# Numbering the rows of a batch by 16 x partition + column, with fewer one-tile loads, in an argmax, gather and scatter kernel

## The chip, the cores and the metric

The kernel runs on one core of one Trainium2 chip. Times are device microseconds of that core, and all runs told here are in the fast state or, where one is a single look, of unknown state. Ratios are the mean time of one kernel's fast runs over the mean of the other's in the same rounds, with a 95% interval, so they are not quite the ratios of the medians quoted beside them. The reported time is about 1.8 us longer than the span of the profile of the same run.

## The reference

```python
B, S, H = 8, 2048, 2560            # scores (B, S, S), values (B, S, H), float32, fixed seed
best_j = np.argmax(scores, axis=2)
gathered = values[b_idx, best_j, :]
out = np.zeros_like(values)
np.add.at(out, (b_idx, best_j), gathered)
```

(The lines are shortened.) Row j of a batch of the output is therefore values[j] times the number of score rows that have their largest element in column j. Rows with a count of 1 are copied, rows with 0 are zeroed, rows with 2 or more are multiplied. In the fixed draw there are 5,875, 6,131 and 4,378 of them over the eight batches.

## The kernel before

VectorE finds the argmax of each row of scores, TensorE counts the columns by one-hot products, and the output is written by indirect DMAs that GpSimd issues, 128 rows each. The count of row j stands in `cnt[p, t]`, at j = 128 t + p.

```python
row_i = consts.tile([P, NT], INT32)                       # row of cnt[p, t]
nc.gpsimd.iota(row_i[:], pattern=[[P, NT]], base=0, channel_multiplier=1)
# ... how many tiles of scores one load takes
most_n = 1 if x < 2 or turn <= x < 3 * NT else 2 if x < 4 or turn <= x < 5 * NT else R
# ... count_steps
lo = am & (P - 1)      # partition p of the count
hi = am >> 7           # column t
# ... rows with count 1: one DMA per column t straight from values to out;
# partitions whose count is not 1 get an index out of bounds and are skipped
def copy_once(t):
    free_running(scatter_rows_in_dram(
        nc, out_flat[:, :], values[b, t * P:(t + 1) * P, :], one_i[:, t:t + 1], last_row))
first = (NT, 6, 4)[min(b, 2)]      # copies issued in a row at the head of a batch
for t in range(first):
    copy_once(t)
# ... rows with 0 and with 2 or more get a rank (running number by partition, then
# column), are put into lists of 128, and list place v goes to the engine v mod 16
def gathers():                      # 5 lists; then scaled by ScalarE and scattered
    for k in range(MCAP):
        gather(v, mi[:, k:k + 1]); scale(v)
        if rest: copy_once(rest.pop(0))
def zeros(columns):                 # 7 lists (12 in the last batch) from a row of zeros
    for k in columns:
        scatter(zrow[:], zi[:, k:k + 1], free_running)
        if rest: copy_once(rest.pop(0))
```

The cuts are marked by dots, and two calls are abbreviated. In the last batch `level_engines` deals the zero rows out so that all sixteen DMA engines get about the same number of row packets in all.

## Time and profile before

| what | before |
|---|---|
| time, median of 4 runs | 827.3 us (826.99 to 827.59) |
| span of the profiled run, whose own time was 829.2 us | 827.4 us |
| moved by DMA | 347.04 MB |
| VectorE busy | 679 us, finished at 697 us |
| row packets (10,240 B) in the trace | 20,762, mean 387.4 ns, median 385 ns |

The lines of the profile stand in the prediction. In the lines with windows the columns are: the window and its length in us, busy us with the number of instructions for each engine, the granted clock, the DMA share of sixteen engines, and GB/s. The trace also records single DMA packets; I call "excess" what packets took beyond the median of their size, summed and divided by 16, which is the time it costs if it falls on all engines alike.

### The profile page before, as it was taken

What the parts mean: (1) busy time and instruction counts of PE and PEld (TensorE: products, weight loads), DVE (VectorE), ACT (ScalarE), POOL (GpSimd) and SP (SyncE); (2) the same over time, 40 slices, a digit from 0 to 9 for tenths busy, and PEclk for the clock granted to TensorE, in tenths of its full rate; (3) what the DMA queues carried; (4) which work ended last, traced back from release to release, by engine and by line L of the source; (5) the groups of instructions that cost most, each with busy time, mean ns of one, the idle gap of its engine ahead of it and who ended that gap; (6) DMA issues with size and microseconds to landing.
All of it is one profiled execution on the core that took longest, in us unless ns stands there. A gap on an engine that the chain in (4) does not pass through costs nothing.

```text
span 827.4 us, 2091 instructions
## 1 busy us (share of the span) xinstructions
PE 14.7 (2%) x273; PEld 14.2 (2%) x273; DVE 679.0 (82%) x794; ACT 100.7 (12%) x43; POOL 273.0 (33%) x277
## 2 busy tenths in 40 slices
PE   0000000000000000000000000000000000000000
PEld 0000000000000000000000000000000000000000
DVE  7999999999999999999999999999999995000000
ACT  1000000320230000230002300002300320230230
POOL 0000641257004141042250140530416365455451
DMA  9999999999999999999999999999999999999996
GB/s 380 437 423 421 404 404 430 424 424 403 425 428 427 428 424 427 427 427 438 418 429 430 425 428 434 417 429 429 435 422 422 423 427 418 425 424 415 423 426 277
DMA packets 48112, 347.04 MB, mean 419 GB/s; under 512 B 19014, under 2 KB 19014, under 8 KB 19014
## 3 DMA queue, kind: packets, MB, share of 16 engines
q0 software_dynamic: 38736, 212.67, 62.0%
q1 hardware_dynamic: 9360, 134.22, 38.1%
q14 instruction: 14, 0.11, 0.0%
q8 instruction: 2, 0.03, 0.0%
HBM read 354.42 MB, written 300.15 MB: 791 GB/s over the span
## 4 chain that ended last, share of the span: by engine, by line
DVE 81%; DMA 12%; issue 3%; POOL 2%; PE 0%; POOLq 0%; DVEq 0%
DVE am L198 37%; DVE mx L197 34%; DMA room<-in_values_dram,many_i 7%; DMA out_dram<-room,many_i 4%; DVE oh_lo L205 3%; DVE oh L332 2%; POOL out_dram L171 1%; POOL out_dram L33 1%; DVE lo L201 1%; DMA room<-in_scores_dram 1%; DVE oh_hi L209 1%; POOL room L166 0%; DVE hi L203 0%; DVE rank L322 0%; DVE put L347 0%
## 5 line engine op out<-in xcount | busy, mean ns | idle before, releaser
L197 DVE MAX8 mx<-room 128x8 f32<-128x2048 f32 x128 | 291.7, 2279 | 4.5 <-DMA room<-in_scores_dram 4.5
L198 DVE FIND_INDEX8 am<-mx,room 128x8 uint32<-128x2048 f32 x128 | 292.5, 2285 | 0.0
L371 ACT ACTIVATE room<-room,many_c 128x2560 f32<-128x2560 f32 x40 | 96.6, 2426 | 694.3 <-DMA room<-in_values_dram,many_i 694.3
L33 POOL DMA_INDIRECT out_dram<-in_values_dram,ones_i x128 | 130.5, 1020 | 130.0 <-DVE m L303 91.6
L171 POOL DMA_INDIRECT out_dram<-room,many_i x40 | 38.9, 974 | 235.9 <-ACT room L371 233.3
L166 POOL DMA_INDIRECT room<-in_values_dram,many_i x40 | 42.7, 1067 | 152.9 <-DMA out_dram<-room,many_i 79.0
L171 POOL DMA_INDIRECT out_dram<-zrow,zero_i x61 | 59.8, 980 | 18.6 <-issue 18.6
L205 DVE TENSOR_TENSOR oh_lo<-lo,lane_f 128x512 bf16<-128x512 uint32 x32 | 22.2, 694 | 0.3
L332 DVE TENSOR_TENSOR oh<-lo,fill_f 128x2048 f16<-128x2048 uint32 x8 | 18.3, 2292 | 0.3
L213 PE MATMUL cnt_ps<-oh_hi,oh_lo 128*128 128x16 bf16 x128 | 8.2, 174 | 572.9 <-DVE oh_hi L209 558.2
L213 PEld LDWEIGHTS <-oh_lo 128*128 128x128 bf16 x128 | 8.4, 105 | 572.7 <-DVE oh_lo L205 571.6
L198 DVE MATCH_VALUE_LOAD am<-mx,room 128x8 f32 x128 | 11.8, 92 | 4.3
L209 DVE TENSOR_TENSOR oh_hi<-hi,lane_f 128x64 bf16<-128x64 uint32 x32 | 7.0, 218 | 0.0
L201 DVE TENSOR_SCALAR lo<-am 128x4 uint32<-128x4 uint32 x32 | 5.7, 177 | 1.1
L350 PE MATMUL l_ps<-put,oh 128*128 128x32 f16 x128 | 4.7, 188 | 73.1 <-DVE put L347 73.1
L350 PEld LDWEIGHTS <-oh 128*128 128x128 f16 x128 | 4.7, 104 | 74.2 <-DVE oh L332 63.8
L203 DVE TENSOR_SCALAR hi<-am 128x4 uint32<-128x4 uint32 x32 | 5.6, 174 | 0.0
L337 DVE TENSOR_TENSOR ez<-hi,lane_f 128x256 f16<-128x256 uint32 x8 | 3.3, 418 | 0.0
L347 DVE TENSOR_TENSOR put<-ez,row_f 128x256 f16<-128x256 f16 x8 | 3.3, 418 | 0.0
L359 DVE TENSOR_SCALAR e<-l_ps 128x32 f32<-128x32 f32 x8 | 1.5, 185 | 2.0 <-PE l_ps L350 2.0
L322 DVE TENSOR_SCALAR rank<-base,off_ps 128x16 f32<-128x16 f32 x16 | 3.0, 232 | 0.0
L345 DVE TENSOR_TENSOR put<-em,row_f 128x128 f16<-128x128 f16 x8 | 2.3, 292 | 0.3
(88 smaller groups left out, 52.5 us busy)
## 6 DMA issues: line engine op xcount, KB each, us to landing
room<-in_scores_dram SPq DMA_DIRECT2D x13, 4096.0 KB, 48.8
room<-in_scores_dram SPq DMA_DIRECT2D x24, 2048.0 KB, 12.3
room<-in_scores_dram SPq DMA_DIRECT2D x28, 1024.0 KB, 10.6
out_dram<-in_values_dram,ones_i POOLq DMA_INDIRECT x128
out_dram<-zrow,zero_i POOLq DMA_INDIRECT x61
room<-in_values_dram,many_i POOLq DMA_INDIRECT x40
out_dram<-room,many_i POOLq DMA_INDIRECT x40
```

The lines of the kernel that those rows point to most:

```text
L33: return eng.add_instruction(ins)
L166: note(nc.gpsimd.indirect_dma_start(out=v, out_offset=None, in_=values_flat[:, :], in_offset=bass.IndirectOffsetOnAxis(ap=idx, axis=0), bo ...
L171: note(nc.gpsimd.indirect_dma_start(out=out_flat[:, :], out_offset=bass.IndirectOffsetOnAxis(ap=idx, axis=0), in_=v, in_offset=None, bound ...
L197: nc.vector.max(out=mx[:], in_=rows)
L198: nc.vector.max_index(out=am[:, g, :], in_max=mx[:], in_values=rows)
L201: nc.vector.tensor_single_scalar(out=lo[:], in_=am[:, :, 0], scalar=P - 1, op=ALU.bitwise_and)
L205: nc.vector.tensor_tensor(out=oh_lo[:], in0=lo[:].unsqueeze(2).to_broadcast([P, G, P]), in1=lane_f[:].unsqueeze(1).to_broadcast([P, G, P]) ...
L209: nc.vector.tensor_tensor(out=oh_hi[:], in0=hi[:].unsqueeze(2).to_broadcast([P, G, NT]), in1=lane_f[:, 0:NT].unsqueeze(1).to_broadcast([P, ...
L213: nc.tensor.matmul(out=cnt_ps[:], lhsT=oh_lo[:, k, :], rhs=oh_hi[:, k, :], start=(t == G - 1 and k == 0), stop=(t == NT - 1 and k == G - 1))
L332: nc.vector.tensor_tensor(out=oh[:], in0=lo[:].unsqueeze(2).to_broadcast([P, NT, P]), in1=fill_f[:].unsqueeze(1).to_broadcast([P, NT, P]), ...
L350: nc.tensor.matmul(out=l_ps[:], lhsT=oh[:, t, :], rhs=put[:, t, :], start=(t == 0), stop=(t == NT - 1))
L371: nc.scalar.activation(out=v, in_=v, func=mybir.ActivationFunctionType.Copy, bias=0.0, scale=mc[:, k:k + 1])
```

## The change

The intent: rows that follow each other in a list should also lie next to each other in memory, the copies should spread over memory, and fewer loads should be of one tile only.

```diff
-    nc.gpsimd.iota(row_i[:], pattern=[[P, NT]], base=0, channel_multiplier=1)
+    nc.gpsimd.iota(row_i[:], pattern=[[1, NT]], base=0, channel_multiplier=NT)
...
-        most_n = 1 if x < 2 or turn <= x < 3 * NT else 2 if x < 4 or turn <= x < 5 * NT else R
+        most_n = 1 if x < 2 or 2 * NT - 2 <= x < 3 * NT - 4 else 2 if x < 4 or turn <= x < 5 * NT else R
...
-  lo: in_=am[:, :, 0], scalar=P - 1, op=ALU.bitwise_and
+  lo: in_=am[:, :, 0], scalar=4, op=ALU.logical_shift_right
-  hi: in_=am[:, :, 0], scalar=7, op=ALU.logical_shift_right
+  hi: in_=am[:, :, 0], scalar=NT - 1, op=ALU.bitwise_and
...
-  nc, out_flat[:, :], values[b, t * P:(t + 1) * P, :], one_i[:, t:t + 1], last_row))
+  nc, out_flat[:, :], values[b].rearrange("(p t) h -> p t h", t=NT)[:, t, :], one_i[:, t:t + 1], last_row))
```

(The lines of `lo`, `hi` and the copy are shortened to what differs; an assertion on the size was added.)

More of the change, by code (lines that the diff above doesn't have):

```diff
@@ L46 @@
     _, _, H = values.shape
-    assert S == S2
+    assert S == S2 and S == 16 * P
     NT = S // P
@@ L200, in count_steps @@
                 lo = small.tile([P, G], U32)
-                nc.vector.tensor_single_scalar(out=lo[:], in_=am[:, :, 0], scalar=P - 1, op=ALU.bitwise_and)
+                nc.vector.tensor_single_scalar(out=lo[:], in_=am[:, :, 0], scalar=4, op=ALU.logical_shift_right)
                 hi = small.tile([P, G], U32)
-                nc.vector.tensor_single_scalar(out=hi[:], in_=am[:, :, 0], scalar=7, op=ALU.logical_shift_right)
+                nc.vector.tensor_single_scalar(out=hi[:], in_=am[:, :, 0], scalar=NT - 1, op=ALU.bitwise_and)
                 oh_lo = small.tile([P, G, P], BF16)
```

## The prediction

> **What bounds the kernel now.** I read the page from the top (busy shares, the slices, the DMA queues), then asked the windows for a table by stage, then the waits, and last counted the trace's records of single DMA packets. The busy shares mislead at first: VectorE is the busiest compute engine, and the chain that ended last is made of its work for 81% of the span. The slices correct that.
>
> ```profile
> span 827.4 us, 2091 instructions
> ...
> DVE  7999999999999999999999999999999995000000
> ...
> DMA  9999999999999999999999999999999999999996
> GB/s 380 437 423 421 404 404 430 424 424 403 425 428 427 428 424 427 427 427 438 418 429 430 425 428 434 417 429 429 435 422 422 423 427 418 425 424 415 423 426 277
> DMA packets 48112, 347.04 MB, mean 419 GB/s; under 512 B 19014, under 2 KB 19014, under 8 KB 19014
> ...
> q0 software_dynamic: 38736, 212.67, 62.0%
> q1 hardware_dynamic: 9360, 134.22, 38.1%
> ```
>
> VectorE is done in slice 34 of 40, about 697 us, and the DMA engines are full in all 39 slices before the last. 62.0 + 38.1 is 100% of the span of sixteen engines. So the bound is DMA engine time: 347 MB at 419 GB/s is 828 us. An engine that waits costs nothing as long as those sixteen stay fed, and the waits say which do wait:
>
> ```profile
> ACT room L371 <- DMA room<-in_values_dram,many_i: 694.3, 35, 144.8
> ...
> POOL room L166 <- DMA out_dram<-room,many_i: 79.0, 18, 20.0
> ...
> DVE mx L197 <- DMA room<-in_scores_dram: 4.5, 1, 4.5
> ```
>
> VectorE waits for a load of scores once in the whole run, the first one. ScalarE and GpSimd wait for DMA, not DMA for them. The windows then show where the engines are full but move less, and where they are not full:
>
> ```profile
> 12.00:60.00 48.00, 0.51 (x8) 0.53 (x8) 47.62 (x40) 0.00 (x0) 0.00 (x0) 1.00 1.00 429
> 60.00:85.00 25.00, 0.52 (x8) 0.56 (x9) 24.34 (x25) 0.00 (x0) 0.00 (x0) 1.00 1.01 422
> ...
> 95.00:110.00 15.00, 0.59 (x16) 0.48 (x15) 14.83 (x17) 0.00 (x0) 11.35 (x13) 1.00 1.02 388
> ...
> 180.00:195.00 15.00, 0.00 (x0) 0.00 (x0) 14.86 (x12) 0.00 (x0) 11.35 (x13) 1.00 1.03 390
> 195.00:600.00 405.00, 8.32 (x152) 8.12 (x152) 399.95 (x428) 48.23 (x20) 118.77 (x119) 1.00 1.01 428
> ...
> 815.00:820.00 5.00, 0.00 (x0) 0.00 (x0) 0.00 (x0) 0.00 (x0) 0.00 (x0) 1.00 0.88 349
> 820.00:827.40 7.40, 0.00 (x0) 0.00 (x0) 0.00 (x0) 0.00 (x0) 0.00 (x0) 1.00 0.20 72
> ```
>
> The last two columns are the DMA share and GB/s. The steady state is 428. Two stretches, 95 to 110 and 180 to 195 us, are full at only 388 to 390: packets take longer there. These are where GpSimd issued runs of single-row copies (sixteen in a row for batch 0, six and then alternating for batch 1). The last 7.4 us are 0.20 full: engines finish at different times.
>
> The packet records give the cost of one packet. Median and mean in ns: one row of 10,240 B 385 and 387.4 (20,762 of them); 8 KiB of scores 309 and 315.2 (3,584); 16 KiB 611 and 614.8 (3,072); 32 KiB 1213 and 1214.6 (1,664); 4-byte completions and skipped rows 9 (19,014). Summed and divided by 16 this is 829 us, a hair over the span since neighbouring packets overlap by about 1%. If every packet took its median, 5.6 us would go: 1.7 of it falls in 85 to 125 us, 1.3 in 180 to 195, 0.5 in the first 12, 2.1 everywhere else.
>
> **What the Trainium skill says.** "Perfetto Trace Analysis", section What "DMA-bound" means: such a kernel is bound by the DMA engines, the issuing sequencer or SBUF reads. The trace says engines: 100% busy, while GpSimd's issues occupy 33% of the span. "HBM Reference", section Specifications: a core alone measures about 425 GB/s, bounded by its sixteen engines, of about 716 GB/s in the domain. The steady 428 agrees. A copy from HBM to HBM uses HBM twice, so a run of copies at full speed would ask for some 850 GB/s by my estimate, above the page's 716; that would explain the 390. "DMA: Bandwidth & Descriptors", Latency and other measured facts: a row pitch in HBM of 512 KiB still gave 207 GB/s per direction, 2 MiB 164, 4 MiB 103. No run here shows pitches that large. The same page's section The descriptor swizzle says which engine serves which SBUF partition; the kernel's lane table, with the packet count checked below, agrees with it.
>
> **The change part by part.** Row numbering becomes 16 x partition + column. VectorE, ScalarE, GpSimd and TensorE keep the same instructions in the same order (I compared the built programs), so only the addresses in DMA and the loads change.
>
> 1. *Loads.* The built program has 16 loads of one tile, 30 of two and 13 of four, in place of 28, 24 and 13. So 12 x 128 = 1,536 packets of 8 KiB become 768 of 16 KiB. By medians (1,536 x 309 - 768 x 611)/16 = 336 ns; by means (1,536 x 315.2 - 768 x 614.8)/16 = 749 ns; six loads fewer save 96 completions of 9 ns, 0.05 us. Gain 0.4 to 0.8 us, take 0.6. VectorE is not fed later in any way that counts: its only wait was at the start, and two-tile loads already follow four-tile ones there.
>
> 2. *Single-row copies.* 5,875 rows are chosen exactly once (counted from the reference's own draw of inputs). Before, one copy took its rows from 128 neighbouring rows, the eight candidates of an engine lying side by side; now they are 160 KiB apart and engines start 1.25 MiB apart. Bytes and packets are the same. At 385 ns the engines spend 5,875 x 385/16 = 141 us on them, so 1% slower packets cost 1.4 us. What can be won is the excess in the two runs of copies, 3.0 us; whether stepping by 16 heals it depends on its cause (HBM bytes: no; neighbouring rows colliding: yes). I take 40%, 1.2 us.
>
> 3. *Lists.* Zero and many rows were listed by partition, so neighbours in a list were 128 rows (1.25 MiB) apart, about six of them per partition; now they are about three rows apart. In 195 to 600 us, where these lists run among loads and copies, 9,026 row packets have only 0.2 us of excess over 16 engines. There is nothing to win. This also bounds the danger in part 2: a 1.25 MiB step over several engines at once already runs at the full rate.
>
> 4. *Balance.* Rows fall to other engines. From the counts of the draw, with the kernel's own levelling arithmetic, row packets per engine before are 1,299 at most (1,284 on the shortest), sum 20,762, which is exactly what the trace has. After: 1,298 at most, 1,292 at least. One packet less, 0.4 us. The draw also stays inside the limits for the overflow path (at most 780 of 896 zeros, 565 of 640 repeats, 62 of 96 at the end), so that path stays untaken.
>
> 5. *End.* The number of running engines falls from 16 at about 818 us to 1 at 825; the last finishes some 4.8 us after the mean. Packet counts were nearly equal, so uneven slow packets cause most of it. Fewer slow packets would bring the slowest forward by a part of that; I book nothing beyond part 2.
>
> Sum: 827.1 - 0.6 - 1.2 - 0.4 = 824.9, rounded to 825.0 us.
>
> **The rivals.** (a) *Strided copies alias in HBM*: all sixteen engines are 1.25 MiB apart in both values and output. If a copy packet took 25% longer, 141 x 0.25 = 35 us, 862 in all. Against it: the lists of before, point 3, and the skill's full rate at a 512 KiB pitch. I give it 4%. (b) *Neighbouring rows were the cause of the slow runs*, and stepping heals them and levels the finish: 3.0 from the packets in both runs and 2 to 3 at the end, with parts 1 and 4 about 820 to 821. For it: slowness sits exactly where copies run alone; against it: the doubled HBM traffic explains that as well. (c) *Nothing but the loads*: HBM bytes are the limit in the bursts, 826. (d) *Two-tile loads starve the engines* before 85 us, where no row transfers fill in: a pair waits for two free buffers. Against it: the singles are kept for tiles 30 to 43, just where the ring catches up with VectorE; each missed microsecond would be one on the end, 828 to 830.
>
> **Range and chances.** The engines are already full and packet medians are those of a fixed rate, so even a kernel without slow packets and with an even finish gains 5.6 + 4.8 = 10.4 us, 1.3%: a gain over 2% (below 810.6) is all but excluded, 2%. A loss over 2% (above 843.6) needs rival (a), 4%. Range 819.5 to 829.5 covers (b), (c) and (d).
>
> **What would show it right or wrong.** Right: DMA at 9 in every slice but the last, 347.0 MB again, 1,536 fewer packets of 8 KiB. Part 1: over 422 GB/s in 60 to 85 us. Part 2: GB/s in the stretches 95 to 110 and 180 to 195 us; 420 or more means (b), 390 again means (c). Rival (a): the q0 share rises well over 62.0% of a longer span, with rows' packets over 400 ns outside the bursts. Rival (d): a DMA digit below 9, or VectorE waiting for scores. The prediction is wrong if the median of row packets is not 385 ns.

## The result

The changed kernel took 829.06 us (median of 4, 828.69 to 830.42) against 827.32 us; the ratio is 1.0024, interval 1.0007 to 1.0042. That is "same" by the 2% rule and inside the predicted range, but it is a small loss where I had put a small gain. The page of the kernel after, from which these lines are, shows what the prediction asked for: DMA at 9 until the last slice, the same bytes, fewer packets.

```profile
span 827.1 us, 2076 instructions
...
DMA  9999999999999999999999999999999999999997
GB/s 382 433 431 423 406 403 428 427 421 404 426 425 428 430 426 425 427 430 429 419 417 436 419 426 431 419 425 430 433 423 412 423 426 418 424 427 417 421 426 304
DMA packets 47248, 347.04 MB, mean 420 GB/s; under 512 B 18918, under 2 KB 18918, under 8 KB 18918
...
q0 software_dynamic: 38736, 212.67, 62.2%
q1 hardware_dynamic: 8496, 134.22, 38.1%
```

The two spans, 827.4 and 827.1 us, are of runs that took 829.2 and 828.9 us: the profiled run of before was slower than its timed ones, so the pair of spans hides the difference of 1.7 us. The windows of the kernel after:

```profile
60.00:85.00 25.00, 0.51 (x8) 0.55 (x9) 24.34 (x25) 0.00 (x0) 0.00 (x0) 1.00 1.00 424
...
95.00:110.00 15.00, 0.59 (x16) 0.48 (x15) 14.83 (x17) 0.00 (x0) 11.34 (x13) 1.00 1.01 381
...
180.00:195.00 15.00, 0.00 (x0) 0.00 (x0) 14.86 (x12) 0.00 (x0) 11.34 (x13) 1.00 1.02 390
195.00:600.00 405.00, 8.29 (x152) 8.09 (x152) 399.94 (x428) 48.37 (x20) 114.48 (x115) 1.00 1.01 426
```

The loads are a little better (424 for 422 GB/s). The two slow stretches have not healed (381 for 388, and 390 again), which by the prediction's own sign is rival (c). The long middle has lost 2 GB/s, although it had nothing to lose to by my account. The mean row packet went from 387.4 to 388.3 ns with the median still 385. Something now slows some row packets, and one profile cannot tell whether copies, lists or the balance of engines do it.

### The profile page after: what moved, and what is told of

It is laid out like the page before. It is cut to its first block, busy times and chain, and to the rows that moved or that the text cites. A ratio compares the mean times of both kernels' runs of the same rounds, so it can differ in the third digit from the quotient of the medians.

```text
span 827.1 us, 2076 instructions
## 1 busy us (share of the span) xinstructions
PE 14.7 (2%) x273; PEld 14.1 (2%) x273; DVE 679.1 (82%) x794; ACT 100.7 (12%) x43; POOL 273.0 (33%) x277
## 4 chain that ended last, share of the span: by engine, by line
DVE 81%; DMA 11%; issue 3%; POOL 2%; PE 0%; POOLq 0%; DVEq 0%
DVE am L198 37%; DVE mx L197 34%; DMA room<-in_values_dram,many_i 7%; DMA out_dram<-room,many_i 4%; DVE oh_lo L205 3%; DVE oh L332 2%; POOL out_dram L171 1%; DVE lo L201 1%; POOL out_dram L33 1%; DMA room<-in_scores_dram 1%; DVE oh_hi L209 1%; DVE rank L322 0%; DVE put L347 0%; DVE ez L337 0%; DVE hi L203 0%
## 5 line engine op out<-in xcount | busy, mean ns | idle before, releaser
L33 POOL DMA_INDIRECT out_dram<-in_values_dram,ones_i x128 | 128.5, 1004 | 141.1 <-DVE m L303 103.0
```

The lines of the kernel that those rows point to most:

```text
L33: return eng.add_instruction(ins)
```

## The experiments

Twelve kernels ran. All but the two measurements with phases were correct.

**1. The parts apart.** Kernel `loads_only` is before with the new rule for loads; `rows_only` is after with the old one.

> The kernel before with only the new rule for the loads (16 loads of one tile, 30 of two). The changed kernel was 1.7 us slower than before. My sum said -0.6 us for this part: 826.7 us. If the theory 'the loads cost it' holds (pairs wait for two free buffers), this kernel alone is 1.5 us or more slower, about 829. If the row numbering costs it, this kernel is 0.4 to 0.8 us faster than before.

> The changed kernel with the old rule for the loads: only the numbering of rows is new. Theory 'loads': equal to before within 0.4 us. Theory 'numbering': 2 to 2.5 us slower than before (1.7 plus the 0.6 that the loads save), about 829.5 us, with row packets that take longer in the trace (mean over 388 ns, against 387.4 before). Theory 'only the uneven finish': row packets of the same mean as before and the difference all after 815 us.

For the next two, copies and lists needed different numberings. The counts are turned into the other numbering by one VectorE product and 16 small matmuls per batch, and ranks and lists use the turned counts (`copies_only` likewise, the other way round):

```diff
+        spread = cnt[p, t] * [t2 == p & 15]
+        for t in range(NT):                    # cl[8 t + (p >> 4), p & 15] = cnt[p, t]
+            nc.tensor.matmul(out=cl_ps[:], lhsT=band[:, 120 - 8 * t:248 - 8 * t], rhs=spread[:, t, :], ...)
-        m[:, 0, :] = cnt == 0;  m[:, 1, :] = cnt >= 2
+        m[:, 0, :] = cl == 0;   m[:, 1, :] = cl >= 2
```

> The numbering of before for the single-row copies and for the loads; only the lists of zero and repeated rows are in order of the row (the counts are turned by 16 small matmuls and one VectorE product per batch, off the path that sets the end). Theory 'stepped copies cost': equal to before within 0.5 us. Theory 'lists in order cost' (neighbouring rows written at the same time by all engines): 2 us or more slower.

> The mirror of the run before: single-row copies step by 16 rows, the lists stay in the old order (rows 128 apart), loads as before. Theory 'stepped copies cost': 2 us or more slower than before, about 829.5 us, with the excess of the row packets at the runs of copies (95 to 125 and 180 to 195 us). Theory 'lists cost': equal to before within 0.5 us. If neither this nor the mirror moves, the cost lies in how rows fall to engines.

All four ran in the same rounds on one chip (before: 828.58 us, 9 runs). The last columns are from the packet records of the one profiled run of each kernel; the first row's are from the profile of before.

| kernel | median us | ratio (95%) | mean row packet ns | excess of row packets us |
|---|---|---|---|---|
| before | 828.58 | | 387.4 | 3.2 |
| loads_only | 828.06 | 0.9997 (0.9983 to 1.0010) | 387.2 | 2.8 |
| lists_only | 829.31 | 1.0009 (0.9995 to 1.0022) | 388.2 | 4.2 |
| copies_only | 832.21 | 1.0043 (1.0029 to 1.0057) | 389.6 | 6.0 |
| rows_only | 831.43 | 1.0044 (1.0030 to 1.0058) | 389.7 | 6.1 |

This settles the part: the stepping copies alone cost 0.43%, as much as the whole new numbering. Lists in order cost nothing clear of noise, and the loads change nothing clear of noise. `lists_only` carries the same extra turning of the counts as `copies_only`, so that work is not the cause. The 2.8 us more excess of `copies_only` makes up most of the 0.43% (3.6 us). The changed kernel itself, in other rounds, lost only 0.24%; the two intervals (up to 1.0042, from 1.0030) overlap, and whether its new loads win back a part is not shown.

**2. Where in time.** GpSimd's transfers go through one queue, so I assumed that they are worked off in their order and gave the n-th row packet to the transfer that the running sum of chosen rows points at (an estimate, since sixteen engines don't run in step). After 200 us, copies have 0.14 us of excess in before and 0.24 in `lists_only`, but 1.15 in the kernel after, 1.56 in `copies_only` and 1.85 in `rows_only`. By this account most of it is where the last copy of one batch and the first four of the next follow each other: these runs of five have 0.04 us in before, 0.85 in the kernel after, 1.25 in `copies_only` and 1.60 in `rows_only`. The copies that alternate with gathers and zero lists, more than twice as many packets, have 0.10 us in before and 0.25 to 0.32 in the three. (The two old stretches before 200 us are not untouched either: row packets have 2.2 us of excess there in before and 3.3 in `copies_only`, but 2.8 in `lists_only` too, so only part of this can be the stepping.) In before, GpSimd issued five copies in a row at 597 to 602 us; with the backlog they move at about 630 to 636. Windows at three such places, of before, of `lists_only`, of `rows_only` and of the kernel after:

```profile
630.00:636.00 6.00, 0.00 (x0) 0.00 (x0) 5.97 (x5) 0.00 (x0) 4.26 (x5) 1.00 1.01 418
...
694.00:702.00 8.00, 0.59 (x16) 0.48 (x15) 2.02 (x14) 0.00 (x0) 6.17 (x7) 1.00 1.02 423
...
762.00:770.00 8.00, 0.00 (x0) 0.00 (x0) 0.00 (x0) 0.00 (x0) 5.95 (x6) 1.00 1.02 423
```

```profile
630.00:636.00 6.00, 0.25 (x4) 0.26 (x4) 5.90 (x12) 0.00 (x0) 4.00 (x4) 1.00 1.01 415
...
694.00:702.00 8.00, 0.96 (x19) 0.64 (x18) 6.46 (x34) 0.00 (x0) 6.17 (x7) 1.00 1.01 417
...
762.00:770.00 8.00, 0.00 (x0) 0.00 (x0) 0.00 (x0) 0.00 (x0) 6.08 (x7) 1.00 1.01 415
```

```profile
630.00:636.00 6.00, 0.00 (x0) 0.00 (x0) 5.97 (x4) 0.00 (x0) 3.66 (x4) 1.00 1.02 379
640.00:690.00 50.00, 1.14 (x15) 0.94 (x15) 48.19 (x76) 12.03 (x5) 23.16 (x24) 1.00 1.01 424
694.00:702.00 8.00, 0.59 (x16) 0.58 (x16) 2.94 (x16) 0.00 (x0) 6.48 (x6) 1.00 1.03 397
704.00:750.00 46.00, 0.00 (x0) 0.00 (x0) 0.00 (x0) 12.13 (x5) 23.01 (x24) 1.00 1.02 424
762.00:770.00 8.00, 0.00 (x0) 0.00 (x0) 0.00 (x0) 0.00 (x0) 5.93 (x7) 1.00 1.01 388
```

```profile
630.00:636.00 6.00, 0.00 (x0) 0.00 (x0) 5.96 (x5) 0.00 (x0) 3.39 (x5) 1.00 1.03 391
...
694.00:702.00 8.00, 0.59 (x16) 0.48 (x15) 2.10 (x15) 0.00 (x0) 6.17 (x7) 1.00 1.02 410
...
762.00:770.00 8.00, 0.00 (x0) 0.00 (x0) 0.00 (x0) 0.00 (x0) 5.94 (x7) 1.00 1.01 415
```

The last column is the one to read. The DMA share is 1.01 to 1.03 everywhere: the engines are never idle. With neighbouring rows the runs of copies move 415 to 423 GB/s, with stepping rows 379 to 397 in `rows_only`, and between the runs (640 to 690, 704 to 750 us) that kernel is at full speed. `copies_only` shows 377, 388 and 385 in the same three windows. The changed kernel itself is milder, 391, 410 and 415, the last no slower than `lists_only`. The windows are narrow and stand at the same times in every kernel, though a run of copies can lie a little earlier or later: over 690 to 702 us before moves 416 and `rows_only` 403. So the place is shown, and the depth of the dip only roughly.

**3. Copies by themselves.** Kernel `phases` drops the argmax and moves whole batches in phases.

> A measurement with a wrong output on purpose: no argmax, every row of a batch taken, eight phases each apart by a wait: 32 copies of neighbouring rows; 32 copies stepping by 16 rows; 32 zero lists in order of the row; 32 zero lists with rows 128 apart; copies and zero lists in turn (neighbouring, then stepping); 32 copies beside 40 loads of scores (neighbouring, then stepping after a spacer of 16 zero lists). Theory 'HBM bytes' (a copy uses HBM twice): copies alone stay clearly below 425 GB/s, both kinds alike within 1%, near 360 to 395, and zero lists run at 420 or more in both orders; copies in turn with zeros run at 420. Theory 'neighbouring rows collide': neighbouring copies at 385 or less, stepping ones at 415 or more. Theory 'stepping aliases': stepping copies at least 3% slower than neighbouring ones, and lists with rows 128 apart slower than lists in order.

The windows of its phases, in order: copies of neighbouring rows, copies stepping by 16, lists in order, the first half of the spread lists, copies of neighbouring rows in turn with zero lists, then copies beside loads (neighbouring, with the spacer; stepping). This profile has no TensorE columns.

```profile
4.00:130.00 126.00, 0.00 (x0) 0.36 (x1) 29.57 (x31) 1.00 0.99 332
133.00:261.00 128.00, 0.00 (x0) 0.00 (x0) 29.65 (x31) 1.00 0.98 327
265.00:366.00 101.00, 0.00 (x0) 0.00 (x0) 29.01 (x30) 1.00 1.00 412
369.00:422.00 53.00, 0.00 (x0) 0.00 (x0) 14.84 (x16) 1.00 1.01 415
...
477.00:681.00 204.00, 0.00 (x0) 0.00 (x0) 60.66 (x63) 1.00 1.00 411
900.00:1148.00 248.00, 0.00 (x0) 0.00 (x0) 45.77 (x48) 1.00 1.00 423
1150.00:1348.00 198.00, 0.00 (x0) 0.00 (x0) 30.27 (x32) 1.00 1.01 424
```

Copies alone move 332 GB/s, which is 664 GB/s of reads and writes together, while the engines are busy 0.99 of the time: their packets take longer (488 ns for a row in the mean). Zero lists, which only write, move 412 or more in either order, and copies beside loads 423. So copies in a row are the one kind of transfer here that is held back, as the "HBM bytes" theory says in kind; in size it missed, with 360 to 395 expected for copies alone and 420 for copies in turn with zeros (411 measured). That the packets wait for memory, and not for something else that only copies use, is argued from these rates and not shown. Stepping copies are 1.9% slower by duration (128.6 for 126.2 us from first to last packet), less than the 3% of the aliasing theory, and seen once. Their mean row packet is only 0.2% longer (489.2 for 488.1 ns); the rest is that the engines were busy 0.98 instead of 0.99 of the time.

The stepping copies in turn with zeros were slower than the neighbouring ones in that run (398 GB/s, leaving out a pause in the phase, against 410, by packet records). The kernel `steps` should have told which side of the copy, read or write, and which distance does it.

> A measurement with a wrong output on purpose: ten phases, each 32 copies of 128 rows in turn with 32 zero lists in order, apart by waits. In the phases before, neighbouring copies in turn with zeros gave 410 GB/s, stepping ones 398. Phases: 1 neighbouring; 2 step 16; 3 reads neighbouring, writes step 16; 4 reads step 16, writes neighbouring; 5 step 2; 6 step 4; 7 writes with engines 128 rows apart and neighbouring rows within an engine; 8 writes with engines on neighbouring rows and steps of 16 within an engine; 9 neighbouring again; 10 step 16 again. Theory 'engines alias': 2 and 3 (or 4) slow, 7 as slow as 3, 8 as fast as 1, step 2 and 4 in between. Theory 'neighbours within an engine help': 8 slow as 3, 7 as fast as 1, step 2 slow already. Theory 'reads': 4 slow and 3 fast. If the difference of 410 and 398 was drift, 9 and 10 do not repeat 1 and 2 within 1%.

It did not tell this, at first sight. All engines stop for about 4 us at 371, 745, 1123, 1498 and 1865 us, and the rate is low from about 5 us before each stop to about 20 us after its beginning. Two phases of step 16 and the repeat of neighbouring rows:

```profile
211.00:371.00 160.00, 0.00 (x0) 0.00 (x0) 46.49 (x48) 1.00 0.99 401
375.00:425.00 50.00, 0.00 (x0) 0.00 (x0) 13.17 (x14) 1.00 0.97 390
...
1696.00:1906.00 210.00, 0.00 (x0) 0.00 (x0) 60.96 (x63) 1.00 0.97 400
1909.00:2112.00 203.00, 0.00 (x0) 0.00 (x0) 60.35 (x63) 1.00 1.00 412
```

The first two lines are phase 2 (stepping), the third is phase 9 (neighbouring), the fourth phase 10 (stepping). The controls do not repeat: from its first to its last packet neighbouring moved 411 and 399 GB/s, stepping 392 and 411, and the slow ones are those with a stop inside. By the rule written beforehand the difference of 410 and 398 was not the order of rows; `phases` has stops of the same kind, at 423 and 796 us, the second of them in that phase.

The packet records say more. In both kernels every stop comes after exactly 113 more indirect transfers (16,272, 32,544 and so on packets of the queue), at whatever time that is. GpSimd runs ahead of the engines: in `steps` it had issued the 113th transfer at 271 us and issued the next only at 373, after the engines had run dry at 371. So the stops belong to the number of transfers issued and not to the order of rows. An engine has 9 packets of each transfer on average, 1,017 of 113 and 1,026 of 114; a list of some 1,020 packets for each engine that is begun anew only when the engines have worked it off would fit, as an estimate, but is not shown. The kernels that do the whole work have no such stop. And the five phases of `steps` without one (neighbouring, reads neighbouring with writes stepping, step 2, writes with engines 128 rows apart, stepping) moved 409 to 413 GB/s, the five with one 388 to 399, the loss lying around the stop. So in turn with zero lists the order of the copies' rows costs nothing above about 1%, seen once. Which side and which distance matter in a run of copies stays open.

**4. Runs of copies made longer and shorter.** `long_near` and `long_step` issue all copies of a batch in one run.

```diff
-        first = (NT, 6, 4)[min(b, 2)]
+        first = NT
```

> The kernel before with all 16 single-row copies of every batch issued in one run (before: 16, 6, then 4 in a row, the rest in turn with gathers and zero lists). Copies alone moved 332 GB/s in the first measurement of phases, against 425 of the engines. Theory 'runs of copies': slower than before by 3 to 15 us, with slices under 400 GB/s at each batch. Theory 'order does not matter': within 1 us of before.

> The same with the new numbering (copies step by 16 rows, loads as before); to be read against its twin with neighbouring rows of the same rounds. Theory 'stepping hurts where copies run alone': about 46 of 128 copies were in such runs when the new numbering cost 3.6 us; with all 128 the difference of the twins grows to 7 to 12 us. Theory 'stepping hurts each copy alike': the difference stays 3 to 4.5 us. Theory 'it is how rows fall to engines': also unchanged, and no more slow packets than in the twin.

The first is before with that one line, the second the changed kernel with it and with the old loads. Both, beside a before of 828.66 us (9 runs): 848.08 us, ratio 1.0232 (1.0218 to 1.0246), and 848.12 us, ratio 1.0236 (1.0222 to 1.0250). Runs of copies do cost, 19 us. Windows of `long_near` and then of `long_step` inside the run of batch 6:

```profile
708.00:712.00 4.00, 0.00 (x0) 0.00 (x0) 0.00 (x0) 0.00 (x0) 3.08 (x4) 1.00 1.05 351
712.00:716.00 4.00, 0.00 (x0) 0.00 (x0) 0.00 (x0) 0.00 (x0) 2.99 (x3) 1.00 1.03 351
716.00:720.00 4.00, 0.00 (x0) 0.00 (x0) 0.00 (x0) 0.00 (x0) 3.00 (x3) 1.00 1.01 338
```

```profile
708.00:712.00 4.00, 0.00 (x0) 0.00 (x0) 0.00 (x0) 0.00 (x0) 3.08 (x4) 1.00 1.04 346
712.00:716.00 4.00, 0.00 (x0) 0.00 (x0) 0.00 (x0) 0.00 (x0) 3.09 (x4) 1.00 1.03 341
716.00:720.00 4.00, 0.00 (x0) 0.00 (x0) 0.00 (x0) 0.00 (x0) 3.08 (x4) 1.00 1.03 343
```

The engines are full and move about 345 GB/s, near the 332 of copies alone, which looks like the same limit inside the real kernel. Over 708 to 728 us they average 353 and 332, so in these profiles the stepping copies are still the slower ones. But my expectation for the twins was wrong. I had written that the difference would grow to 7 to 12 us, and in the time it vanished; the theory "each copy alike" (3 to 4.5 us) missed as well. In a long run neighbouring rows hit the limit nearly as hard as stepping ones. In the one profile of each, row packets had 17.1 and 21.0 us of excess, the average engine finished at 837.3 and 841.4 us and the last at 842.7 and 843.8, so the neighbouring kernel lost most of its lead in an uneven finish. But its profiled run (846.27 us) was the fastest of its five, 1.8 us under their median, and the other's (848.12) was the median. With one profile each, why the twins tie is not shown.

The kernel with shorter runs was first tried on neighbouring rows with the new loads, then on the changed kernel:

```diff
-        first = (NT, 6, 4)[min(b, 2)]
+        first = (8, 4, 4)[min(b, 2)]
```

> The numbering of before, the new rule for loads, and shorter runs of single-row copies: 8 in a row for batch 0 in place of 16, 4 in place of 6 for batch 1, the others in turn with lists and gathers. If the slow stretches at 95 to 125 and 180 to 195 us come from copies alone in a row, up to 2 us go and the time is 1.5 to 2.5 us under before with the loads' part, and the GB/s there exceed 400. If they come from anything else issued at that time, no change beyond the loads' 0.3 us.

> The changed kernel with shorter runs of copies (8 in a row for batch 0, 4 for batch 1). With neighbouring rows this gave 1.0 us less than before. Theory 'runs': part of the loss of the numbering goes with the runs, so it comes out between the two: 828 to 829.5 where before has 827.6, that is 2 us or less over the kernel with neighbouring rows and short runs. Theory 'each copy alike': 3.5 us over that one, 830 or more.

`mixed_early`: 826.53 us against 827.57, ratio 0.9987 (0.9973 to 1.0000). The stretch at 180 to 195 us rose from 390 to 423 GB/s, the one at 95 to 110 us did not rise (377, before 388). Half of the expectation held. In the first stretch the excess of row packets did halve with the run (0.46 us for 0.92), but that of the load packets rose (0.96 for 0.22), so the length of the run does not alone explain it; the rest stays open. Nor is the second healed by the runs alone for certain: `loads_single` below kept its run of six copies and had only 0.2 us of excess between 180 and 200 us, against 1.3 in before.

`mixed_step`: 832.10 us against 828.66, ratio 1.0042 (1.0028 to 1.0055), as slow as the new numbering with old runs and loads; its own base, the changed kernel, had 1.0024 in other rounds, and the intervals overlap. So shorter early runs gave no gain that can be seen. It looks like the theory "each copy alike", but the test was badly aimed: it shortened the runs of batches 0 and 1, while the runs of five copies at the later boundaries, where step 2 had found the cost, are unchanged in it. Its windows there show 376, 392 and 377 GB/s. It agrees with the place; what speaks against "each copy alike" is the small excess of the alternating copies in step 2 and the phases of step 3 without a stop, not this run.

**5. The loads, made large.** `loads_single` takes every load as one tile.

```diff
-        most_n = 1 if x < 2 or turn <= x < 3 * NT else 2 if x < 4 or turn <= x < 5 * NT else R
+        most_n = 1
```

> The kernel before with every load of scores one tile (128 loads of 1 MiB), to make the cost of small load packets large enough to measure. From the packet times of the trace before: 3,072 packets of 16 KiB become 6,144 of 8 KiB, +3,072 x 7/16 ns = 1.3 us; 1,664 of 32 KiB become 6,656 of 8 KiB, +1,664 x 23/16 ns = 2.4 us; 63 more loads with 16 completions of 9 ns, 0.6 us: +4.3 us, 0.5%, if the engines' time per packet is what counts. If small loads cost more than that (or starve the engines), more; if loads are hidden, 0.

829.66 us against 827.57, ratio 1.0027 (1.0013 to 1.0041), so 2.2 us where 4.3 were expected. Smaller loads do cost, but half of the sum: row packets had 1.9 us of excess instead of 3.2 in before, and 16 and 32 KiB packets, which had 0.9 us, are gone. So the cost per packet is there, and the whole sum is only half confirmed, because other packets got faster; the 0.4 to 0.8 us for the real change of loads is below what `loads_only` could show.

**6. A version under both.** `mixed_more` keeps the numbering of before, takes the new loads, and breaks up the runs at the later boundaries as well:

```diff
-        first = (NT, 6, 4)[min(b, 2)]
+        first = (8, 2, 2)[min(b, 2)]
...
             scatter(staged[k], mi[:, k:k + 1], ...)
+            if b > 0 and k >= MCAP - 2 and rest:
+                copy_once(rest.pop(0))
```

> A try at a version under both kernels: numbering of before, the new loads, 8 copies in a row for batch 0 and 2 for every later batch, the two that are left over following the last two scatters of gathered rows. If runs cost, it is another 0.3 to 1 us under the kernel with 8, 4, 4 (which was 0.13% under before), so about 0.2% under before. If the engines run dry while GpSimd waits for a scatter, it is slower than that one.

826.21 us against 828.66, ratio 0.9972 (0.9959 to 0.9986), as expected: a quarter of a per cent under before, and the lowest ratio of all kernels here. Mean row packet 386.1 ns. What of this is due to the runs and what to the loads is not told apart. Whether the stepping copies would also be free with runs as short as these was not run and stays open.

## Why the prediction was right or wrong, point by point

The frame held. DMA engine time sets the end, the engines stay full, the bytes and median packet times do not change, and so neither a gain nor a loss of 2% came. The measured 829.06 us lies in the range of 819.5 to 829.5 near its upper edge; the direction was wrong. That it lies inside owes something to luck: the upper edge was put there for rival (d), starved engines, which did not happen, while the kind of loss that did happen, rival (a), was put at 862.

1. *Loads* (taken as -0.6 us): `loads_only` gave 0.9997, that is -0.2 us with an interval of -1.4 to +0.8. Not contradicted, not shown. Rival (d), starved engines, is refused by the full DMA slices.
2. *Single-row copies* (taken as -1.2 us): this is the step that failed, in its sign. `copies_only` measured +3.6 us. The weighing of 40% for a healing treated it, in the sum, as "heals or does nothing"; stepping made the short runs of copies slow that had been free (0.04 us of excess became 0.85 to 1.60), and did not heal the two old stretches (381 and 390 GB/s in the kernel after, 375 and 384 in `rows_only`).
3. *Lists* (taken as 0): right, 1.0009 with 1 inside the interval. But the conclusion drawn from it, that lists with rows 1.25 MiB apart bound the danger for the copies, was the faulty support of step 2. Lists move at 412 to 415 GB/s in both orders, whereas copies alone are limited to 332: what is harmless for a kind of transfer that is not held back need not be so for one that is. The sentence "No run here shows pitches that large" also overlooks that the old lists' 1.25 MiB lies between the skill's 512 KiB and 2 MiB.
4. *Balance* (taken as -0.4 us): the packet count agreed with the trace (20,762), which checks the sum and not the split over the engines; no run isolates this term, and it is smaller than the intervals.
5. *End* (booked as nothing): the unevenness did not carry the loss. In the profile of `rows_only` the average engine finished 3.3 us later than in that of before and the last one 1.8 us later (827.4 for 825.6), so the loss is engine time, and a more even finish hid a part of it in that pair of profiles.

Of the rivals, (a) came true in kind and at a tenth of the size feared: slower copy packets, not 25% on all of them but 6 to 9% fewer GB/s in the narrow windows on the short runs of `rows_only`, and 2 to 6% in those of the kernel after. What is behind it, aliasing or lost neighbours, is not told apart. Rival (b) is refuted. Rival (c) named a limit that fits the rates, that copies use memory twice, but not the loss.

## What to carry to other kernels

When the DMA engines are full, ask of each kind of transfer how often it crosses the memory. Copies from memory to memory cross twice; here they lost speed in a row (332 GB/s, for 423 beside loads), and only in short runs of them did the order of rows show. So mix such copies with loads or with stores from SBUF rather than issuing them in a row. Evidence that an address pattern is harmless must come from the same kind of transfer, issued in the same company. And before testing "shorter runs", look up in the trace which runs carry the cost.

## What the Trainium skill lacked or had wrong

- "HBM Reference", Specifications, gives about 425 GB/s for a core streaming alone and about 716 GB/s per domain, but no rate for copies within HBM; the row pitch entry named in the next point has one, 214 GB/s per direction as the full rate of 16 KiB rows. Here copies alone, of 10 KiB rows issued by GpSimd, moved 332 GB/s in each direction, 664 of reads and writes together, with the engines 0.99 busy; zero lists 412 to 415, copies beside loads 423.
- "DMA: Bandwidth & Descriptors", Latency and other measured facts, has row pitches from 512 KiB up for 16 KiB rows in large tiles. It lacks sparse row copies: at 160 KiB from row to row (1.25 MiB from engine to engine) they cost the kernel 0.43%, and most of what the copies' packets lost after 200 us lies in runs of copies.
- The same page, Specifications, gives about 27 GiB/s per engine. Packets of 32 KiB took 1213 ns, 27.0 GB/s or 25.2 GiB/s; sixteen of them are 432 GB/s, which fits the page's own 435 GB/s, so the unit should be GB/s.
- No page has the stops of about 4 us that come after every 113 indirect transfers when GpSimd issues them far ahead of the engines (`steps` and `phases`), or the low rate just after them.
